# A rotary embedding on one core: one load and one store sent as sixteen interleaved partial DMAs

## The chip, the cores and the metric

The kernel runs on 1 core of one Trainium2 chip. The metric is the device time of one execution in microseconds (us); the median of 3 runs of the kernel before is 316.16 (316.1 to 316.17).

## The reference

x has 8 sequences of 2048 positions, 16 heads and 64 values a head, in float32 (8.39 MB a sequence). Neighbouring values of a head make pairs, and each pair is turned by an angle that depends on the position alone:

```python
x_pairs = x.reshape(batch, seq_len, num_heads, head_dim // 2, 2)
x1 = x_pairs[..., 0]
x2 = x_pairs[..., 1]
...
out1 = x1 * cos - x2 * sin
out2 = x1 * sin + x2 * cos
out = np.stack([out1, out2], axis=-1).reshape(batch, seq_len, num_heads, head_dim)
```

Everything is read once and written once: 67 MB in, 67 MB out.

## The kernel before

A sequence is called a row, b = 0 to 7. Its 2048 positions are spread over the 128 partitions, 16 positions to each, so that a partition holds 16 x 1024 values of a row: 64 KB as float32 in memory, 32 KB as bfloat16 in the tile `xt`. `xt` has five slots of a row each; `HOME` gives the slot of each row: rows 0 to 4 have slots 0 to 4, rows 5, 6 and 7 take slots 0, 1 and 2 again.

`load(b, n)` and `store(b, n)` move n rows that stand in neighbouring slots, in one DMA issued from POOL (GpSimd). These DMAs also convert: loads from float32 to bfloat16, stores back. `rotate(b)` turns a row in place with three operations of DVE (VectorE): `qt` = row x sine table (L89), row = row x cosine table (L92), row = row + `qt` with neighbours swapped (L97). There is one `qt`, so rotations follow one another.

The order is written out by hand. POOL issues the loads of rows 0, then 1 and 2, then 3 and 4. Row 0 goes out when row 2's first multiply is done (two tiny ACT copies, L120 and L121, see to that). POOL then copies one element of slot 4 (`mark`, L126), which holds it until load(3, 2) has landed; then come store(1, 2), load(5, 1), load(6, 2), store(3, 2) and store(5, 2). Each of these waits in POOL's order for what it needs: a load into a used slot waits for the landing of the store that empties the slot, a store waits for its rotations. The framework places these waits, from the parts of tiles that each instruction reads and writes, with semaphores; the DMAs of POOL take eight of them in turn.

The last row's output is converted to float32 by ACT (ScalarE) in four casts (L138) into `wide`, which lies over slots 3 and 4, and is stored by a DMA from SP (L139), on a queue of its own. The first quarter of row 0 also comes over SP's queue, as float32, and is cast by ACT.

Of the kernel before, what the change touches and what calls it, by code (L numbers as in the profile page):

```python
# [2 lines left out]

# [4 lines left out]


@with_exitstack  # L10
def kernel(
    ctx: ExitStack,
    tc: tile.TileContext,
    x: bass.AP,
    cos: bass.AP,
    sin: bass.AP,
    out: bass.AP,
):
    nc = tc.nc
    fp32 = mybir.dt.float32  # L20
    bf16 = mybir.dt.bfloat16
    mult = mybir.AluOpType.mult
    add = mybir.AluOpType.add

    B, S, H, D = x.shape
    P = 128
    K = S // P
    KP = 16
    D2 = D // 2
    HD = H * D  # L30
    NX = 5
    HEAD = 4
    PART = 4
    STAGE = 3


    HOME = [0, 1, 2, 3, 4, 0, 1, 2]

    x_t = x.rearrange("b (p k) h d -> b p k (h d)", p=P, k=K)
    out_t = out.rearrange("b (p k) h d -> b p k (h d)", p=P, k=K)  # L40
    x_r = x.rearrange("b (p k) h d -> p b (k h d)", p=P, k=K)
    out_r = out.rearrange("b (p k) h d -> p b (k h d)", p=P, k=K)
    cos_t = cos.rearrange("(p k) c -> p (k c)", p=P, k=K)
    sin_t = sin.rearrange("(p k) c -> p (k c)", p=P, k=K)

    consts = ctx.enter_context(tc.tile_pool(name="consts", bufs=1))
    stage = ctx.enter_context(tc.tile_pool(name="stage", bufs=1))

    xt = consts.tile([P, NX, K * HD], bf16)
    cos_sb = consts.tile([P, K * D2], fp32)  # L50
    sin_sb = consts.tile([P, K * D2], fp32)
    c_tab = consts.tile([P, K, D], bf16)
    s_tab = consts.tile([P, K, D], bf16)

    wide = (
        xt[:, STAGE : STAGE + 2]
        .rearrange("p a c -> p (a c)")
        .bitcast(fp32)
        .rearrange("p (k c) -> p k c", c=HD)
    )  # L60

    gate = consts.tile([1, 1], bf16)
    mark = consts.tile([1, 1], bf16)

    def home(b, k0=0, k1=K):
        return xt[:, HOME[b], k0 * HD : k1 * HD].rearrange("p (k c) -> p k c", c=HD)

    def load(b, n):
        h = HOME[b]
        nc.gpsimd.dma_start(out=xt[:, h : h + n], in_=x_r[:, b : b + n])  # L70

    def store(b, n):
        h = HOME[b]
        nc.gpsimd.dma_start(out=out_r[:, b : b + n], in_=xt[:, h : h + n])  # L74

    def rotate(b, k0=0, k1=K, between=None):
        nk = k1 - k0
        xp = home(b, k0, k1)
        qt = stage.tile([P, KP, HD], bf16, name="qt", tag="work")

        def rows(a):
            return a.rearrange("p k (h e) -> p k h e", h=H, e=D)

        def tab(a):
            return dataclasses.replace(
                a, offset=a.offset + k0 * D, ap=[a.ap[0], [D, nk], [0, H], [1, D]]
            )

        nc.vector.tensor_tensor(out=rows(qt[:, :nk]), in0=rows(xp), in1=tab(s_tab), op=mult)  # L89
        if between is not None:  # L90
            between(qt)
        nc.vector.tensor_tensor(out=rows(xp), in0=rows(xp), in1=tab(c_tab), op=mult)  # L92
        q_swap = dataclasses.replace(
            qt, offset=qt.offset + 1, ap=[qt.ap[0], [2, nk * HD // 2], [-1, 2]]
        )
        x3 = xp.rearrange("p k (a j) -> p (k a) j", j=2)
        nc.vector.tensor_tensor(out=x3, in0=x3, in1=q_swap, op=add)  # L97

    with tc.manual_schedule():
        head = stage.tile([P, HEAD, HD], fp32, name="st", tag="work")  # L100
        nc.sync.dma_start(out=head[:, :HEAD], in_=x_t[0, :, :HEAD])
        nc.gpsimd.dma_start(out=home(0, HEAD), in_=x_t[0, :, HEAD:])  # L102
        nc.gpsimd.dma_start(out=cos_sb, in_=cos_t)  # L103
        nc.gpsimd.dma_start(out=sin_sb, in_=sin_t)  # L104
        load(1, 2)
        load(3, 2)

        nc.scalar.copy(out=home(0, 0, HEAD), in_=head[:, :HEAD])  # L108
        s2 = s_tab.rearrange("p k (i j) -> p (k i) j", j=2)
        nc.vector.tensor_copy(out=s2[:, :, 0], in_=sin_sb)  # L110
        nc.vector.tensor_scalar_mul(s2[:, :, 1], sin_sb, -1.0)  # L111
        nc.vector.tensor_copy(  # L112
            out=c_tab.rearrange("p k (i j) -> p (k i) j", j=2),
            in_=cos_sb.to_broadcast([P, K * D2, 2]),
        )
        rotate(0, 0, HEAD)
        rotate(0, HEAD, K)

        def first_store(qt):
            nc.scalar.copy(out=gate, in_=qt[:1, KP - 1, HD - 1 :])  # L120
            nc.scalar.copy(out=xt[:1, HOME[0], :1], in_=xt[:1, HOME[0], :1])  # L121
            store(0, 1)

        rotate(1)
        rotate(2, between=first_store)
        nc.gpsimd.tensor_copy(out=mark, in_=xt[:1, 4, K * HD - 1 :])  # L126
        store(1, 2)
        load(5, 1)
        load(6, 2)
        rotate(3)  # L130
        rotate(4)
        store(3, 2)
        for b in range(5, B):
            rotate(b)
            if b == 6:
                store(5, 2)
        for k in range(0, K, PART):
            nc.scalar.copy(out=wide[:, k : k + PART], in_=home(B - 1, k, k + PART))  # L138
        nc.sync.dma_start(out=out_t[B - 1], in_=wide)  # L139


# [1 line left out]
_INS = ['x', 'cos', 'sin']  # L143
_OUTS = [((8, 2048, 16, 64), 'float32')]


# [23 lines left out]
```

## Time and profile before

| | us |
|---|---|
| median of 3 runs | 316.16 |
| the profiled execution, its span | 314.3 |
| DVE busy | 210.3 (67%) |
| ACT busy | 19.3 (6%) |
| POOL busy | 12.4 (4%) |
| DVE waits for loads of x (L89), 3 times | 34.3 in total |
| POOL waits for stores to land before it issues loads (L70), twice | 43.1 in total |
| one DVE operation on a row | 8.69 |
| share of the DMA queue of POOL, of SP | 92.1%, 8.0% |

The slices of the page cut the span into 40 stretches of 7.9 us; a digit is the busy share in tenths. Issuing a DMA takes POOL some 0.55 to 0.72 us, counted from when it no longer waits; the transfer itself is not POOL's work. The GB/s of the page count the bytes where they land: a load counts 2 bytes a value, a store 4.

### The profile page before, as it was taken

To read this page: it belongs to the slowest core of one execution; us is meant where nothing else is said; L and a number is where in the kernel's file an instruction comes from. 1 tells how busy PE (TensorE), PEld (TensorE's weight loads), DVE (VectorE), ACT (ScalarE), POOL (GpSimd) and SP (SyncE) were. 2 spreads that over 40 slices of the span, in tenths; PEclk is the share of its full clock that TensorE was granted. 3 is DMA by queue.
4 is the path that set the end of the run, shared out by engine and by line. 5 is a ranking of instruction groups with operands and counts; after the bars stand their busy time and mean duration, and the time that the engine had idled before them with its cause. 6 is when DMAs were issued, how large, how long until landed. Compare 5 with 4: busy or idle time off the path is not lost.

```text
span 314.3 us, 114 instructions
## 1 busy us (share of the span) xinstructions
DVE 210.3 (67%) x30; ACT 19.3 (6%) x8; POOL 12.4 (4%) x16
## 2 busy tenths in 40 slices
DVE  0009995099999999999992299903999999200000
ACT  1030000000000000000000000000000000790000
POOL 4000000000002400000000000000000000000000
DMA  7999999999999999999999999999999999999996
GB/s 253 264 284 200 200 200 267 200 200 204 263 200 267 409 525 400 400 425 509 400 200 225 242 200 200 234 234 334 400 509 425 400 400 525 409 400 400 525 409 267
DMA packets 2512, 102.24 MB, mean 325 GB/s; under 512 B 208, under 2 KB 208, under 8 KB 336
## 3 DMA queue, kind: packets, MB, share of 16 engines
q0 software_dynamic: 2224, 91.75, 92.1%
q1 hardware_dynamic: 288, 10.49, 8.0%
HBM read 67.63 MB, written 67.11 MB: 429 GB/s over the span
## 4 chain that ended last, share of the span: by engine, by line
DVE 67%; another core or an unknown queue 11%; ACT 3%; ACTq 1%; issue 0%; DVEq 0%
DVE xt L92 22%; DVE xt L97 22%; DVE qt L89 22%; ACT xt L138 3%; ACTq L165 1%; DVE c_tab L112 0%; DVEq L89 0%; DVEq L92 0%
## 5 line engine op out<-in xcount | busy, mean ns | idle before, releaser
L89 DVE TENSOR_TENSOR qt<-xt,s_tab 128x16384 bf16<-128x16384 bf16 (+2 forms) x9 | 69.7, 7743 | 34.5 <-DMA xt<-in_x_dram 34.3
L92 DVE TENSOR_TENSOR xt<-xt,c_tab 128x16384 bf16<-128x16384 bf16 (+2 forms) x9 | 69.7, 7743 | 0.4
L97 DVE TENSOR_TENSOR xt<-xt,qt 128x16384 bf16<-128x16384 bf16 (+2 forms) x9 | 69.7, 7743 | 0.3
L138 ACT CAST xt<-xt 128x4096 f32<-128x4096 bf16 x4 | 14.1, 3601 | 171.7 <-DVE xt L97 171.7
L110 DVE CAST s_tab<-sin_sb 128x512 bf16<-128x512 f32 x1 | 0.5, 454 | 23.8 <-DMA sin_sb<-in_sin_dram 23.8
L74 POOL DMA_DIRECT2D out_dram<-xt x4 | 2.7, 670 | 184.9 <-ACT xt L121 93.4
L126 POOL COPY mark<-xt 1x1 bf16<-1x1 bf16 x1 | 5.0, 5019 | 2.6 <-DMA xt<-in_x_dram 2.6
L120 ACT COPY gate<-qt 1x1 bf16<-1x1 bf16 x1 | 0.2, 192 | 78.6 <-DVE qt L89 78.6
L70 POOL DMA_DIRECT2D xt<-in_x_dram x4 | 2.7, 696 | 43.1 <-DMA out_dram<-xt 43.1
L108 ACT CAST xt<-st 128x4096 bf16<-128x4096 f32 x1 | 3.6, 3605 | 13.1 <-DMA st<-in_x_dram 13.1
L108 ACT ACT_TABLE_LOAD x1 | 1.3, 1283 | 0.7 <-PEq L154 0.7
L102 POOL DMA_DIRECT2D xt<-in_x_dram x1 | 0.7, 680 | 0.8 <-PEq L165 0.8
L112 DVE CAST c_tab<-cos_sb 128x1024 bf16<-128x1024 f32 x1 | 0.7, 685 | 0.0
L103 POOL DMA_DIRECT2D cos_sb<-in_cos_dram x1 | 0.6, 569 | 0.0
L104 POOL DMA_DIRECT2D sin_sb<-in_sin_dram x1 | 0.6, 562 | 0.0
L111 DVE TENSOR_SCALAR s_tab<-sin_sb 128x512 bf16<-128x512 f32 x1 | 0.4, 444 | 0.0
L121 ACT COPY xt<-xt 1x1 bf16<-1x1 bf16 x1 | 0.2, 188 | 0.0
L154 POOL MEMSET const-float32-0.0<- 128x1 f32 x1 | 0.1, 99 | 0.2 <-issue 0.2
L154 POOL MEMSET const-bfloat16-1.0<- 128x1 bf16 x1 | 0.1, 102 | 0.0
L154 POOL MEMSET const-float32-1.0<- 128x1 f32 x1 | 0.1, 99 | 0.0
L154 POOL MEMSET const-uint8-127<- 128x1 uint8 x1 | 0.1, 99 | 0.0
## 6 DMA issues: line engine op xcount, KB each, us to landing
xt<-in_x_dram POOLq DMA_DIRECT2D x3, 8192.0 KB, 59.3
xt<-in_x_dram POOLq DMA_DIRECT2D x1, 4096.0 KB, 57.6
xt<-in_x_dram POOLq DMA_DIRECT2D x1, 3072.0 KB, 21.1
st<-in_x_dram SPq DMA_DIRECT2D x1, 2048.0 KB, 14.4
cos_sb<-in_cos_dram POOLq DMA_DIRECT2D x1, 256.0 KB, 21.2
sin_sb<-in_sin_dram POOLq DMA_DIRECT2D x1, 256.0 KB, 21.3
out_dram<-xt POOLq DMA_DIRECT2D x4, 49.9
out_dram<-xt SPq DMA_DIRECT2D x1, 30.0
```

Of the source, the lines that this page charges most:

```text
L70: nc.gpsimd.dma_start(out=xt[:, h : h + n], in_=x_r[:, b : b + n])
L74: nc.gpsimd.dma_start(out=out_r[:, b : b + n], in_=xt[:, h : h + n])
L89: nc.vector.tensor_tensor(out=rows(qt[:, :nk]), in0=rows(xp), in1=tab(s_tab), op=mult)
L92: nc.vector.tensor_tensor(out=rows(xp), in0=rows(xp), in1=tab(c_tab), op=mult)
L97: nc.vector.tensor_tensor(out=x3, in0=x3, in1=q_swap, op=add)
L102: nc.gpsimd.dma_start(out=home(0, HEAD), in_=x_t[0, :, HEAD:])
L103: nc.gpsimd.dma_start(out=cos_sb, in_=cos_t)
L108: nc.scalar.copy(out=home(0, 0, HEAD), in_=head[:, :HEAD])
L112: nc.vector.tensor_copy(out=c_tab.rearrange("p k (i j) -> p (k i) j", j=2), in_=cos_sb.to_broadcast([P, K * D2, 2]),)
L126: nc.gpsimd.tensor_copy(out=mark, in_=xt[:1, 4, K * HD - 1 :])
L138: nc.scalar.copy(out=wide[:, k : k + PART], in_=home(B - 1, k, k + PART))
L165: with _tile.TileContext(nc) as tc:
```

## The change

The load of rows 6 and 7 in one DMA, `load(6, 2)`, and the store of rows 3 and 4 in one DMA, `store(3, 2)`, are taken apart. Row 6 is loaded in 8 DMAs of 16 partitions each, and row 3 is stored in 8 such DMAs; part g takes the partitions g, g + 8, g + 16 and so on. Load parts and store parts are issued in turn, after rotate(3) in the program's order. Row 7's load follows them as a DMA of its own, and row 4's store follows rotate(4). Nothing else changes; in the changed kernel the lines from `rotate` on stand 10 lines further down, and those behind the edit 13.

```diff
--- before.py
+++ after.py
@@ -73,6 +73,16 @@
         h = HOME[b]
         nc.gpsimd.dma_start(out=out_r[:, b : b + n], in_=xt[:, h : h + n])
 
+    G = 8
+
+    def load_part(b, g):
+        h = HOME[b]
+        nc.gpsimd.dma_start(out=xt[g::G, h], in_=x_r[g::G, b])
+
+    def store_part(b, g):
+        h = HOME[b]
+        nc.gpsimd.dma_start(out=out_r[g::G, b], in_=xt[g::G, h])
+
     def rotate(b, k0=0, k1=K, between=None):
         nk = k1 - k0
         xp = home(b, k0, k1)
@@ -126,10 +136,13 @@
         nc.gpsimd.tensor_copy(out=mark, in_=xt[:1, 4, K * HD - 1 :])
         store(1, 2)
         load(5, 1)
-        load(6, 2)
         rotate(3)
+        for g in range(G):
+            load_part(6, g)
+            store_part(3, g)
+        load(7, 1)
         rotate(4)
-        store(3, 2)
+        store(4, 1)
         for b in range(5, B):
             rotate(b)
             if b == 6:
```

## The prediction

> **What bounds the kernel now.** I read the page's slices first, then the timeline around the edit, then stretches of the span between two landings, then the issues with their time to landing.
>
> ```profile
> DVE  0009995099999999999992299903999999200000
> ...
> DMA  7999999999999999999999999999999999999996
> ...
> HBM read 67.63 MB, written 67.11 MB: 429 GB/s over the span
> ```
>
> The DMA engines are busy in every slice; DVE has holes and ends long before the span does. So the transfers set the time, and DVE only has to feed the last store early enough.
>
> ```profile
> 101.04 5.02 POOL L126 COPY mark<-xt 1x1 bf16<-1x1 bf16 x1 [2.58 <-DMA xt<-in_x_dram]
> ...
> 132.29 8.69 DVE L97 TENSOR_TENSOR xt<-xt,qt 128x16384 bf16<-128x16384 bf16 x1
> 141.01 8.69 DVE L89 TENSOR_TENSOR qt<-xt,s_tab 128x16384 bf16<-128x16384 bf16 x1
> ...
> 159.44 0.70 POOL L70 DMA_DIRECT2D xt<-in_x_dram  x1 [38.20 <-DMA out_dram<-xt]
> 167.52 0.72 POOL L74 DMA_DIRECT2D out_dram<-xt  x1 [7.37 <-DVE xt L97]
> 178.39 8.69 DVE L89 TENSOR_TENSOR qt<-xt,s_tab 128x16384 bf16<-128x16384 bf16 x1 [11.17 <-DMA xt<-in_x_dram]
> ...
> 216.95 8.69 DVE L89 TENSOR_TENSOR qt<-xt,s_tab 128x16384 bf16<-128x16384 bf16 x1 [12.42 <-DMA xt<-in_x_dram]
> ...
> 243.13 8.69 DVE L89 TENSOR_TENSOR qt<-xt,s_tab 128x16384 bf16<-128x16384 bf16 x1
> 243.40 0.70 POOL L74 DMA_DIRECT2D out_dram<-xt  x1 [75.16 <-DVE xt L97]
> ...
> 269.31 14.12 ACT L138 CAST xt<-xt 128x4096 f32<-128x4096 bf16 x4 [171.70 <-DVE xt L97]
> 283.46 0.35 SPq L139 DMA_DIRECT2D out_dram<-xt  x1
> ```
>
> The starts give the landings, since each waits for one: load(3, 2) at 101.04, store(1, 2) at 159.44, load(5, 1) at 178.39, load(6, 2) at 216.95. rotate(4) is the DVE line at 141.01: today it follows rotate(3) at once.
>
> ```profile
> 62.40:101.04 38.64, 38.48 (x5) 0.29 (x2) 0.56 (x2) 1.00 1.01 231
> ...
> 101.04:216.95 115.91, 91.89 (x11) 0.00 (x0) 7.71 (x5) 1.00 1.01 326
> 283.46:293.30 9.84, 0.00 (x0) 0.00 (x0) 0.00 (x0) 1.00 1.00 426
> ```
>
> Columns: stretch, its length, busy DVE, ACT, POOL, clock, DMA share, GB/s. Two rows loaded take 38.64, 19.32 a row. Three rows stored and three loaded take 115.91, again 19.32, with one turn from loads to stores and one back inside. Turning costs nothing and wins nothing.
>
> **The parts themselves.** A part is an eighth of a row: 19.32 / 8 = 2.41 us. Sixteen take 38.6, what the load of the seventh row and the store of the fourth take today. No row shows a DMA of 16 partitions, nor loads and stores in turn. Bounds for a pair, 4.83 as two parts in a row: below, a load's packet is 64 KB read and 32 KB written and a store's the reverse (the GB/s column counts the landing side: 231 for loads, 426 for stores, at one pace), so with both sides running apart a pair needs 96/128 of that, 3.62. Above, if only half of the engines or half of the landing width worked at a time, 9.66. I take 4.83 plus 2 x 0.03: the six rows took 115.91 - 3 x 38.64, nothing, over their two turns, and 0.03 allows for an error of reading. Sixteen parts: 0.4 more at most.
>
> **Issuing them.** One POOL instruction of 0.70 becomes 16, plus a load(7, 1) of its own; one store (3, 2) becomes store(4, 1). In the built program POOL's DMAs take eight semaphores in turn, and each waits for the DMA eight before it. At 159.44 seven parts go out, 7 x 0.7 = 5 us; the eighth waits for load(5, 1), at 178.39, and what stands behind it on POOL is only parts and load(7, 1). The DMA queue holds 7 x 2.41 = 16.9 us of parts then, so each later issue, a landing every 2.41, stays well ahead. Cost nothing; load(7, 1) goes out when the ninth part lands, 178.4 + 9 x 2.41 = 200.1, ahead of its turn at 217. If that cover were gone, each issue would show its 0.7 and a start.
>
> **The wait that is added.** In the built program rotate(4)'s first multiply, which reads row slot 4 alone, now waits for semaphores 4, 2, 6 and 0 at a count of 48: three DMAs each, and the third on each is a load part of the seventh row, the last four of them. Its second multiply waits for the last four store parts likewise. Neither shares a byte with slot 4; the framework takes the strided parts for overlapping. Before, these two waited for DVE and for the mark alone. Behind the waiting instruction stand all of rotate(4) to rotate(7) on DVE, and for them wait store(4, 1), store(5, 2), the ACT casts and SP's last store.
>
> The last load part is the fifteenth: 178.4 + 15 x 2.41 + 0.4 = 215.0. The last store part lands at 217.4, before the first multiply is done (215.0 + 8.7), so it adds nothing. A rotation takes 243.13 - 216.95 = 26.18. Four end at 215.0 + 4 x 26.18 = 319.7, where today the last ends at 269.3: 50.4 later. ACT and its hand-over take 283.46 - 269.31 = 14.15: SP's store is issued at 333.9.
>
> Today that store meets the tail of store(5, 2) and takes 30.0 to land. Now store(4, 1) goes out at 215.0 + 26.2 + 0.3 = 241.5 and store(5, 2) at 215.0 + 3 x 26.18 + 0.3 = 293.8, each onto idle engines.
>
> ```profile
> 1.50:1.75 0.25, 0.00 (x0) 0.25 (x1) 0.25 (x1) 1.00 0.56 131
> ...
> 5.50:6.00 0.50, 0.00 (x0) 0.00 (x0) 0.00 (x0) 1.00 2.97 639
> ```
>
> SP's first issue at 0.74 shows its first traffic about 1.0 us later. POOL's first, at 1.25, joins at the latest at 5.5, so a cold start of POOL's is 1 to 4.2 us. store(5, 2) then lands by 293.8 + (1 to 4.2) + 38.6 + 0.7, 334.1 to 337.3 (0.7 from the last byte to the landing is an estimate: the first row, L102 and the head together, lands at 1.25 + 21.1 = 22.35, 20.6 after the first traffic at 1.74, where a row is 19.3; half of the 1.3 over). SP's store alone: 333.9 + 1.0 + 19.3 + 0.7 = 354.9; with POOL's tail left over, all 24 eighths end 2.4 x 24 after the first packet, at the latest 293.8 + 4.2 + 57.9 + 0.7 = 356.6. I take 355.2. From the last landing (283.46 + 30.0 = 313.46) to the end of the span are 0.8: span 356.0. The median of the runs is 316.16 against the profile's 314.3, 1.86 beside the span: 357.8. In short +41.6: DVE +50.4, less the 9 us by which the last store no longer shares its engines.
>
> **Rivals.**
> Half pace (15%): the parts of one DMA use half the engines or half the width. For it: no row shows such a shape. Against: a load fills only half of the landing width. Full price 15 x 2.41 = 36.2 before rotate(4) starts, 394; a quarter of it 367. The Trainium skill, "SBUF — State Buffer", section on the DMA port swizzle, says that bandwidth depends on how many of 16 ports the partitions reach; every eighth partition reaches 8 by its formula. No run so far shows it.
>
> A start for every part (2%): if each part began as cold as SP's first DMA, 1.0 us, the last load part would land 15 us later: 372.8. Against: the six rows above came in five DMAs of one queue without a gap, and 16.9 us of parts are queued. The Trainium skill, "DMA: Bandwidth & Descriptors", section "Anatomy of one DMA", gives each DMA a fixed cost of some 2.0 us, most of it waiting for the last write's receipt; by it an estimate would add 30 us, 388. The trace agrees for a cold start at most.
>
> Both directions at once (8%): pairs at 3.62 instead of 4.83. For it: a load leaves half of the write side free. Against: two turns in 115.91 us saved nothing. Seven pairs ahead of the last load part: 7 x 1.21 = 8.5, 349.3. Even this cannot win: all parts together last 38.6, and the wait costs 41.
>
> The wait is not there in effect (5%), the other side: if each of the four counts were met by the first DMA on its semaphore (load(3, 2), a table, store(1, 2), the first load, all landed by 159.44), rotate(4) would start at 141 as now. Engines stay full, and the time is 316.2 + 0.4 = 316.6; with directions overlapping, 8 x 1.21 less, 306.9. For it: only the program's listing, no trace, has the wait. Against: the count is 48, three DMAs. It decides as soon as rotate(4) starts before 178.
>
> **How the numbers follow.** The forecast has 70% and its own range is 355 to 361, from POOL's start and 0.4 of turns. The range is taken from 349, the whole overlap, to 366, almost a quarter of the half pace; left out are the rival without the wait, the starts and most of the half pace, about 19%. Less than 0.2%, 0.6 us, is no change here. Faster 3% and same 2% are the last rival's two ends; slower 95%.
>
> **What would show it.** DVE idle from 141 to about 215 before rotate(4)'s first multiply, released by a load part; DMA slices empty near 236 to 243 and 263 to 295; an unchanged 38.6 us for the parts; ACT casts from about 320. I am wrong if rotate(4) starts at 141, or if the parts take far from 38.6.

## The result and the profile after

The changed kernel takes 357.31 us (median of 4 runs, 357.28 to 357.36) against 316.17 for the kernel before (316.1 to 316.27): 1.1301 times, with a 95% interval of 1.1288 to 1.1314. The profiled execution has a span of 355.5, against 314.3.

The slices of the page of the changed kernel, each 8.9 us long, and its HBM line:

```profile
DVE  0039980999999998000000008999999999990000
...
DMA  8999899899899899999999999848920008998988
...
HBM read 67.63 MB, written 67.11 MB: 379 GB/s over the span
```

The same bytes move, but DVE has one hole of eight slices, and behind it the DMA engines have a hole of their own, which they never had before. The timeline shows where both begin and end:

```profile
132.36 8.69 DVE L107 TENSOR_TENSOR xt<-xt,qt 128x16384 bf16<-128x16384 bf16 x1
159.84 0.52 POOL L80 DMA_DIRECT2D xt<-in_x_dram  x1 [38.58 <-DMA out_dram<-xt]
...
178.56 0.49 POOL L84 DMA_DIRECT2D out_dram<-xt  x1 [15.32 <-DMA xt<-in_x_dram]
...
200.48 0.57 POOL L70 DMA_DIRECT2D xt<-in_x_dram  x1 [1.93 <-DMA xt<-in_x_dram]
214.91 8.69 DVE L99 TENSOR_TENSOR qt<-xt,s_tab 128x16384 bf16<-128x16384 bf16 x1 [73.86 <-DMA xt<-in_x_dram]
223.69 8.69 DVE L102 TENSOR_TENSOR xt<-xt,c_tab 128x16384 bf16<-128x16384 bf16 x1
...
241.41 0.54 POOL L74 DMA_DIRECT2D out_dram<-xt  x1 [40.37 <-DVE xt L107]
...
293.83 0.74 POOL L74 DMA_DIRECT2D out_dram<-xt  x1 [51.88 <-DVE xt L107]
...
319.75 14.12 ACT L151 CAST xt<-xt 128x4096 f32<-128x4096 bf16 x4 [222.06 <-DVE xt L107]
333.89 0.35 SPq L152 DMA_DIRECT2D out_dram<-xt  x1
```

rotate(4)'s first multiply, at 141.01 before, starts at 214.91. The bracket says what ended its 73.86 us of idle time: a load of x. Row 4 has been in slot 4 since 101.1, row 5's load landed before 178.56, and row 7's load stands in the queue behind the parts, so this can only be a load part of row 6. Everything that hangs on DVE follows late: store(4, 1) at 241.41, store(5, 2) at 293.83, the casts at 319.75 and SP's store at 333.89. What that does to the DMA engines is in the stretches (length, busy DVE, ACT, POOL, clock, DMA share, GB/s):

```profile
178.40:217.10 38.70, 2.19 (x1) 0.00 (x0) 4.96 (x10) 1.00 1.02 325
...
236.30:245.00 8.70, 8.60 (x2) 0.00 (x0) 0.54 (x1) 1.00 0.46 196
...
262.00:295.00 33.00, 32.86 (x5) 0.00 (x0) 0.74 (x1) 1.00 0.00 0
```

The sixteen parts themselves run about as fast as two whole rows did, 38.7 us with the engines full. (No row shows the landing at which that stretch ends. From 178.56 to 200.48, both released by landings, nine parts took 2.44 each, which would make 39.0 for sixteen.) The loss comes after: some 6 us of emptiness before store(4, 1) and 33 before store(5, 2), 39 of the 41.1 us.

### The profile page after: what moved, and what is told of

It reads as the page before. It is cut to its first block, busy times and chain, and to the rows that moved or that the text cites. A ratio compares the mean times of both kernels' runs of the same rounds, so it can differ in the third digit from the quotient of the medians.

```text
span 355.5 us, 139 instructions
## 1 busy us (share of the span) xinstructions
DVE 210.3 (59%) x30; ACT 19.3 (5%) x8; POOL 19.9 (6%) x32
## 4 chain that ended last, share of the span: by engine, by line
DVE 52%; DMA 27%; ACT 3%; another core or an unknown queue 3%; ACTq 1%; POOL 1%; issue 1%; DVEq 0%; POOLq 0%
DVE xt L102 17%; DVE xt L107 17%; DVE qt L99 17%; DMA xt<-in_x_dram 15%; DMA out_dram<-xt 12%; ACT xt L151 3%; ACTq L178 1%; POOL xt L80 0%; POOL out_dram L84 0%; DVE c_tab L122 0%; DVEq L99 0%; DVEq L102 0%; POOLq L80 0%
## 5 line engine op out<-in xcount | busy, mean ns | idle before, releaser
L74 POOL DMA_DIRECT2D out_dram<-xt x4 | 2.5, 636 | 194.8 <-DVE xt L107 101.2
L80 POOL DMA_DIRECT2D xt<-in_x_dram x8 | 3.9, 491 | 46.3 <-DMA out_dram<-xt 38.6
L84 POOL DMA_DIRECT2D out_dram<-xt x8 | 3.9, 493 | 23.2 <-DMA xt<-in_x_dram 15.3
L70 POOL DMA_DIRECT2D xt<-in_x_dram x4 | 2.6, 664 | 6.8 <-DMA out_dram<-xt 4.9
L112 POOL DMA_DIRECT2D xt<-in_x_dram x1 | 0.7, 670 | 0.8 <-PEq L178 0.8
```

The lines of the kernel that those rows point to most:

```text
L80: nc.gpsimd.dma_start(out=xt[g::G, h], in_=x_r[g::G, b])
L84: nc.gpsimd.dma_start(out=out_r[g::G, b], in_=xt[g::G, h])
```

## The experiments

All times are medians, ratios are to the kernel before run beside them, with a 95% interval. The theory: the wait that the framework puts before rotate(4), because it takes the strided parts for overlapping slot 4, is the whole loss. Its rivals: the new order, the parts themselves, taking turns.

**Whole rows in the new order.** It undoes the parts and leaves the order.

```diff
-        for g in range(G):
-            load_part(6, g)
-            store_part(3, g)
+        load(6, 1)
+        store(3, 1)
         load(7, 1)
```

> The order of the change with whole rows: row 6 loaded, row 3 stored, row 7 loaded, row 4 stored, each in one DMA of 128 partitions. In the program rotate(4) waits for no DMA of these. Theory A (the wait on the strided parts is the whole loss): rotate(4) starts at 141, the DMA engines never stop, 316.2 us within 0.4. Theory B (the new order, with row 4's store later and more DMAs, costs by itself): over 320.

Measured: 316.28 us, 1.0001 (0.9992 to 1.001). The timeline of this kernel:

```profile
140.98 8.69 DVE L99 TENSOR_TENSOR qt<-xt,s_tab 128x16384 bf16<-128x16384 bf16 x1
...
204.50 8.69 DVE L99 TENSOR_TENSOR qt<-xt,s_tab 128x16384 bf16<-128x16384 bf16 x1
...
276.63 0.35 SPq L151 DMA_DIRECT2D out_dram<-xt  x1
```

rotate(4) is back at 140.98 and rotate(6), at 204.50, even starts 12 us earlier than before, since row 6 lands alone. SP's store goes out 7 us earlier, and nothing is won: the DMA queue is full to the end either way. The order is free, so theory B falls here.

**The wait alone.** The kernel before, with one element of row 6 copied by DVE ahead of rotate(4).

```diff
+    hold = consts.tile([1, 1], bf16)
...
         rotate(3)
+        nc.vector.tensor_copy(out=hold, in_=xt[:1, 1, :1])
         rotate(4)
```

> The kernel before with its two-row DMAs, and one copy of one element of row 6 by DVE ahead of rotate(4), so that rotate(4) waits for load(6, 2) as it does for the parts in the changed kernel. Theory A: rotate(4) starts at 217.1; four rotations of 26.18 end at 321.8, casts and hand-over 14.15, store 20.7, end 0.84 and 1.86 beside the span: 359.4. Theory B (the parts carry the loss): 316.2 to 320.

Measured: 359.3 us, 1.1365 (1.1349 to 1.138). The one-element copy in the timeline:

```profile
216.87 0.14 DVE L132 COPY hold<-xt 1x1 bf16<-1x1 bf16 x1 [75.94 <-DMA xt<-in_x_dram]
216.94 8.67 DVE L90 TENSOR_TENSOR qt<-xt,s_tab 128x16384 bf16<-128x16384 bf16 x1
...
335.90 0.35 SPq L141 DMA_DIRECT2D out_dram<-xt  x1
```

Without a single part, a wait in the same place costs the same and 2.0 more. That is where its release lies: 216.9 here, when two rows have landed, 214.9 in the changed kernel.

**The parts alone.** The same sixteen parts of every eighth partition in turn, but slots 0, 1 and 2, 3 and 4 in three tiles, and rotate(4) ahead of the parts.

```diff
-    xt = consts.tile([P, NX, K * HD], bf16)
+    xa = consts.tile([P, 1, K * HD], bf16)
+    xb = consts.tile([P, 2, K * HD], bf16)
+    xc = consts.tile([P, 2, K * HD], bf16)
+    SLOT = [(xa, 0), (xb, 0), (xb, 1), (xc, 0), (xc, 1)]
...
         rotate(3)
+        rotate(4)
         for g in range(G):
             load_part(6, g)
             store_part(3, g)
         load(7, 1)
-        rotate(4)
...
-                store(5, 2)
+                store(5, 1)
+                store(6, 1)
```

> The same sixteen parts of every eighth partition in turn, but the slots lie in three tiles (0; 1 and 2; 3 and 4) and rotate(4) stands ahead of the parts, so that no rotation shares a tile with parts that it does not need. Row 5 and row 6 are stored by a DMA each. Theory A: the wait is gone, the parts take 2.433 us as in the changed kernel, 0.02 more than packets within a DMA: 316.2 + 16 x 0.02 = 316.5, up to 316.9. Theory B (parts in turn cost engines or POOL something that the empty DMA time of the changed kernel hid): over 318. Theory C (loads and stores overlap): 306.9 to 315.

Measured: 316.6 us, 1.0011 (1.0003 to 1.002). Rows 4, 5 and 6 begin their rotations at

```profile
140.99 8.69 DVE L103 TENSOR_TENSOR qt<-xc,s_tab 128x16384 bf16<-128x16384 bf16 x1
...
178.44 8.69 DVE L103 TENSOR_TENSOR qt<-xa,s_tab 128x16384 bf16<-128x16384 bf16 x1 [11.24 <-DMA xa<-in_x_dram]
...
214.97 8.69 DVE L103 TENSOR_TENSOR qt<-xb,s_tab 128x16384 bf16<-128x16384 bf16 x1 [10.38 <-DMA xb<-in_x_dram]
```

and only row 6 waits for the parts, as it must, until 214.97. All sixteen parts are there, in turn, and cost 0.4 us. Nothing is won by them either: theory C falls.

**rotate(4) ahead of the parts, in one tile.** The changed kernel, with only the line moved:

```diff
         rotate(3)
+        rotate(4)
         for g in range(G):
...
         load(7, 1)
-        rotate(4)
```

> The changed kernel with rotate(4) ahead of the parts in the program. rotate(5), the first rotation behind the parts, then takes the wait on them. Theory A: rotate(4) at 141, rotate(5) at 215.0; three rotations end at 293.6, casts and hand-over to 307.7, store 20.7, end 0.84, 1.86 beside the span: 331.1, that is one rotation of 26.2 less than the changed kernel. If the wait were bound to slot 4 and not to the first rotation behind the parts: 316.5.

Measured: 331.16 us, 1.0471 (1.0453 to 1.049). The next rotation in the program takes the wait over, as the starts of rotate(4) and rotate(5) show:

```profile
141.06 8.69 DVE L99 TENSOR_TENSOR qt<-xt,s_tab 128x16384 bf16<-128x16384 bf16 x1
...
215.15 8.69 DVE L99 TENSOR_TENSOR qt<-xt,s_tab 128x16384 bf16<-128x16384 bf16 x1 [47.88 <-DMA xt<-in_x_dram]
```

It is not slot 4 that is held: rotate(5), which works on slot 0, waits for the parts just as rotate(4) did. So the first rotation behind the parts pays, whichever of the two slots it touches. In three tiles, with the same order, rotate(5) did not wait for them (178.44). One rotation saved is 26.15 us, 357.31 - 331.16, where a rotation takes 26.18.

**Load parts first, then store parts.** This tells the two waits of rotate(4) apart.

```diff
         for g in range(G):
             load_part(6, g)
+        for g in range(G):
             store_part(3, g)
```

> The changed kernel with all eight load parts issued first and then all eight store parts. Theory A: rotate(4)'s first multiply waits for the last load part, at 178.4 + 8 x 2.43 = 197.9, and its second, by the program, for the last store part, at 217.4; that second wait, hidden in the changed kernel, now sets the start: rotate(4) ends at 217.4 + 17.45 = 234.9 in place of 241.1, and the time is 357.3 - 6.2 = 351.1. If only the load parts held rotate(4): 17 less than the changed kernel, 340.3. The sixteen parts take 38.9 as before if turning between loads and stores neither costs nor wins; 38.6 if the 0.02 a part was the turning.

Measured: 351.57 us, 1.1114 (1.1096 to 1.1132). The timeline of rotate(4):

```profile
198.91 8.69 DVE L99 TENSOR_TENSOR qt<-xt,s_tab 128x16384 bf16<-128x16384 bf16 x1 [57.98 <-DMA xt<-in_x_dram]
...
218.15 8.69 DVE L102 TENSOR_TENSOR xt<-xt,c_tab 128x16384 bf16<-128x16384 bf16 x1 [10.55 <-DMA out_dram<-xt]
```

The first multiply is let go 16 us earlier, by the last load part, and then the second waits 10.55 for a store part. The second wait, for which the changed kernel shows nothing, is as real as the first; there it is covered by the first multiply. From the issue that row 5's landing released, at 179.06 in this run, to the last store part's landing are 39.1 us, 2.44 a part. That is no less than the 2.44 of the nine parts in turn, so the turning is not seen to cost the 0.02 us a part.

**16 neighbours to a part.** Only the choice of partitions changes.

```diff
-        nc.gpsimd.dma_start(out=xt[g::G, h], in_=x_r[g::G, b])
+        nc.gpsimd.dma_start(out=xt[16 * g : 16 * g + 16, h], in_=x_r[16 * g : 16 * g + 16, b])
...
-        nc.gpsimd.dma_start(out=out_r[g::G, b], in_=xt[g::G, h])
+        nc.gpsimd.dma_start(out=out_r[16 * g : 16 * g + 16, b], in_=xt[16 * g : 16 * g + 16, h])
```

> The changed kernel with one thing changed: a part takes 16 neighbouring partitions, 16 g to 16 g + 15, not every eighth. In the program rotate(4) then waits for no part. Theory A: 316.5 as the three tiles, if a part still takes 2.43 us. Theory D (parts slow down when their partitions lie close together, which the Trainium skill's page SBUF - State Buffer would have for 4 of 16 ports): a part of 4.83 us adds 38.6 us of transfers, 355; only partly so, between 318 and 355.

Measured: 330.83 us (329.67 to 332.18), 1.0473 (1.0445 to 1.05). rotate(4) is at 141.07: the framework sees that neighbours in slots 1 and 3 leave slot 4 alone, so it was the stride that it could not see through. But the time isn't 316.5, and the pace of the parts lies between theory A's and theory D's. The last load part lands at 228.95, where rotate(6) starts; the stretch up to there:

```profile
178.40:228.95 50.55, 26.07 (x3) 0.00 (x0) 5.50 (x11) 1.00 0.99 251
```

In 50.55 us the engines are busy throughout and move fifteen parts, 3.37 each on average instead of 2.43. The mishap that I had feared for every eighth partition, parts at a lower pace, exists for 16 neighbours. The average hides two paces, as POOL's issues in the same run show, each released by a landing:

```profile
178.55 0.49 POOL L84 DMA_DIRECT2D out_dram<-xt  x1 [15.83 <-DMA xt<-in_x_dram]
183.25 0.49 POOL L80 DMA_DIRECT2D xt<-in_x_dram  x1 [4.21 <-DMA xt<-in_x_dram]
185.83 0.49 POOL L84 DMA_DIRECT2D out_dram<-xt  x1 [2.10 <-DMA out_dram<-xt]
```

After row 5's landing the first load part takes 4.7 us to land, and the store part behind it 2.6; in the pairs that follow it is 4.2 to 4.5 and 2.0 to 2.4. The loads are the slow ones.

**Neighbours, loads first and then stores.** The two edits before this one together:

```diff
         for g in range(G):
             load_part(6, g)
+        for g in range(G):
             store_part(3, g)
...
-        nc.gpsimd.dma_start(out=xt[g::G, h], in_=x_r[g::G, b])
+        nc.gpsimd.dma_start(out=xt[16 * g : 16 * g + 16, h], in_=x_r[16 * g : 16 * g + 16, b])
```

and the same in `store_part`.

> The kernel with 16 neighbouring partitions to a part, with all load parts first and then all store parts; rotate(4) waits for no part. Theory D (a part of 16 neighbours is held by its few ways into SBUF, each direction for itself, so that the mixture of loads and stores in the run before spread the load): parts of 4.83 us in one direction, 316.2 + 16 x 2.41 = 354.8. Theory F (the slowness of 14 us belongs to the shape, whatever the direction): about 330.8 again. Theory G (it came from taking turns): 316.5.

Measured: 334.69 us, 1.0574 (1.0534 to 1.0614). None of the three theories had this number. The stretches of the load parts and of most of the store parts:

```profile
178.76:215.18 36.42, 26.08 (x4) 0.00 (x0) 3.88 (x8) 1.00 0.99 130
215.33:235.00 19.67, 19.60 (x3) 0.00 (x0) 1.59 (x3) 1.00 1.01 400
```

Eight load parts take 36.42, 4.55 each, 1.9 times a part of whole-row pace, and land 130 GB/s by this view where loads before landed 231. The store parts run at 400 GB/s by the view, where stores before ran at 426. How long they take can be estimated from the starts of rotate(6), at 215.18, and rotate(7), each released by the landing of its row:

```profile
254.46 8.69 DVE L99 TENSOR_TENSOR qt<-xt,s_tab 128x16384 bf16<-128x16384 bf16 x1 [13.14 <-DMA xt<-in_x_dram]
```

Between the two landings are 39.28 us, for eight store parts and row 7's load. With 19.3 for the load, 20.0 are left, 2.5 a store part. So the shape slows loads, into SBUF, and hardly stores, out of it; with 8 x (4.55 - 2.41) = 17.1 the time would be 333.4, and with 0.7 for the stores 334.1. Theory D was right for one direction only. And here taking turns does win something: in turn the same parts took 330.83.

**Four times as many turns.** The three-tile kernel with each part cut in four along the row.

```diff
-        nc.gpsimd.dma_start(out=t[g::G, h], in_=x_r[g::G, b])
+        c = slice(q * W, q * W + W)
+        nc.gpsimd.dma_start(out=t[g::G, h, c], in_=x_r[g::G, b, c])
...
         for g in range(G):
-            load_part(6, g)
-            store_part(3, g)
+            for q in range(Q):
+                load_part(6, g, q)
+                store_part(3, g, q)
```

> The three-tile kernel with each part cut in four along the row: 64 DMAs of 16 KB an engine, load and store in turn, so four times as many turns. Theory A (a DMA of its own costs an engine 0.02 us, turning wins nothing): 64 x 0.02 = 1.3 over 316.2, 317.5. Theory C (finer turns overlap reading and writing): below 316, at best 306.9. Theory E (POOL's issuing binds: 0.5 us an issue and as much to wake for each wait against 0.6 us of transfer): 64 us in place of 38.6, up to 342.

Measured: 317.91 us, 1.005 (1.0034 to 1.0066). The stretch of the parts:

```profile
178.40:217.90 39.50, 25.97 (x3) 0.00 (x0) 29.44 (x60) 1.00 1.08 321
```

Sixty-four DMAs cost 317.91 - 316.27 = 1.6 us, 0.026 each, and no overlap appears at 16 KB either. POOL is busy for 29.44 of the 39.5 us, so it keeps up, with little left.

## Why the prediction came out right

*The bound.* That the transfers set the time, and DVE only has to feed the last store, is what the whole-row run shows: DVE 7 us earlier at the end, no change in the time.

*The parts.* Taken at 2.41 us and 0.03 for the turn; the fifteen up to the last load part took 214.91 - 178.56 = 36.4, 2.42 each. That the 0.4 us allowed in all fits what was measured is luck: it stood for an error of reading over the turns, and the runs show it as a small cost of each DMA that does not go away without the turns. The upper bound, half pace, was not reached by every eighth partition; 16 neighbours came within 6% of it, in loads. The lower bound, both directions at once, never showed: with every eighth partition, parts in turn take as long as parts not in turn at 64 KB, and four times as many turns at 16 KB win nothing over whole rows.

*Issuing.* Hidden as said. The size was off to the good side: an issue of a part took 0.49, not 0.7. The order of waits was as said: the eighth part at 178.56, released by row 5's load; load(7, 1) at 200.48 (said: 200.1).

*The wait.* Said: rotate(4) at 215.0, DVE's end at 319.7, SP's store issued at 333.9. Measured: 214.91, 319.7, 333.89. That the store parts' wait would be covered by the first multiply was right, and the run with loads first shows what it costs without that cover.

*The tail.* POOL's cold start was the unknown, 1 to 4.2 us. The stretches right after its two late issues:

```profile
241.41:242.50 1.09, 1.09 (x1) 0.00 (x0) 0.54 (x1) 1.00 0.00 0
...
293.83:295.10 1.27, 1.27 (x1) 0.00 (x0) 0.74 (x1) 1.00 0.00 0
295.10:296.10 1.00, 1.00 (x1) 0.00 (x0) 0.00 (x0) 1.00 2.43 1049
```

It took 1.1 to 1.3 us, the low end of a range that the earlier trace could not narrow. By the prediction's own sum store(5, 2) then ends at 334.4, before the first traffic of SP's store (334.7), and that store landed 20.7 after its issue (said: 21.0), against 30.0 before. The view of the issues has it:

```profile
out_dram<-xt SPq DMA_DIRECT2D x1, 20.7
```

So the allowance of 0.3 for a POOL tail left over, and the 0.3 by which SP's store landed sooner than said, make up the 0.5 by which 357.8 was too high.

*The sums.* The two parts of the loss, 50.4 on DVE and 9 given back because SP's store has the engines to itself, came out as 319.72 - 269.29 = 50.4 and 30.0 - 20.7 = 9.3.

*The rivals.* Half pace: refuted for this shape; for 16 neighbours nearly true of the loads and not of the stores. A start for every part: 0.02 instead of 1.0. Both directions at once: refuted for this shape in the changed kernel, in three tiles and in quarter packets. The wait without effect: refuted by rotate(4)'s start at 214.91; the copy of one element shows the same price without the parts.

## What to carry to other kernels

Before slicing a tile by a stride over partitions, look in the built program at what the instructions behind the slice wait for: a framework that follows tiles by their ranges may hold every user of the tile, and the price is that of the first one in program order, all of the queue behind it included. Give what is sliced a tile of its own, and put ahead of the parts what shares that tile and need not wait (the kernel with three tiles did both). Or slice so that ranges stay apart, but then look at the pace of the transfers: 16 neighbouring partitions were slower to load here. With the DMA engines full and each part at full pace, mixing loads and stores in one queue won nothing in this kernel.

## What the runs showed of the hardware that was not expected

Parts of 16 neighbouring partitions load at 4.55 us each, while the same parts store at an estimated 2.5, close to full pace, and parts of every eighth partition do both at 2.42 to 2.44.

The Trainium skill, "SBUF — State Buffer", section on the DMA port swizzle, ties the pace to the number of ports that the partitions reach; by its formula 16 neighbours reach 4 of 16 and every eighth partition 8. Its table has some 109 GB/s for 4 ports and some 218 for 8 as what long transfers come to. For loads the runs come close to both figures: eight load parts of 16 neighbours landed a row's 4.19 MB in 36.42 us, 115 GB/s, and eight of every eighth partition, at 2.42 us each, land it at 217 GB/s. For stores they do not: eight store parts of 16 neighbours took the same 4.19 MB out of SBUF in some 20.0 us, 210 GB/s. No run here tells why.

Whether the ports are what slows these loads is not shown either. Sixteen neighbouring partitions are also one unbroken piece of x in memory, about 1 MB, where every eighth partition takes pieces of 64 KB from all over the row. Both changed together, and no run changes one alone.

A DMA of its own costs an engine 0.02 to 0.03 us while the queue is full: 0.4 us for the sixteen parts in three tiles (316.6 against 316.22) and 1.6 for the sixty-four (317.91 against 316.27). Without turns between loads and stores the pace was the same 2.44 us a part, so the change of direction is not seen to be the cost.
